# A sparse 3x3 convolution: TensorE's loop body cut to two blocks, input rows copied into two fixed tiles, both images in one add

## The chip, the cores and the metric

The kernel runs on one core of one Trainium2 chip. The metric is the device time of one execution in microseconds (us), from several executions; a profile is taken of one of them. The page of a profile gives a span, from the first to the last instruction on the core, and the device time of the same execution is a little longer than that span.

The engines are called by the names of the profile: PE is TensorE (matmuls; PEld are its weight loads), DVE is VectorE, ACT is ScalarE, POOL is GpSimd, SP is SyncE, which here only issues DMAs. SBUF is the on-chip memory, PSUM the eight accumulator banks that PE writes. A name with a q at its end (SPq, PEq, DVEq) is an engine's sequencer, which issues instructions, waits on semaphores and runs loops.

## The reference

The input holds 16 images of 64 channels and 64x64 points, the weight 128x64x3x3, about 90% of it zero. The output is a plain 3x3 convolution with a border of zeros, in float32:

```python
x_pad = np.pad(x, ((0, 0), (0, 0), (pad, pad), (pad, pad)), mode='constant')
...
if weight[co, ci, kh, kw] != 0:
    output[b, co] += weight[co, ci, kh, kw] * x_pad[b, ci, kh:kh+h, kw:kw+w]
```

The kernel treats the weight as dense. The input is 16.8 MB in float32, the output 33.6 MB, and all of both passes through the core's DMA engines.

## The kernel before

**Tiling.** Two images lie side by side on the 128 partitions (64 channels each): a pair. There are NP = 8 pairs. A block is 16 output rows of a pair, so there are NB = 32 blocks, four to a pair. PE works on both images of a block at once: each product is issued as two matmuls with 64 rows of the array each (`n = 0, 1` in `product`), one for each image, and they run side by side.

**The arithmetic.** Write G0, G1, G2 for the three rows of the filter. For an even output row r and the odd row below it, with S = x[r] + x[r+1] and P = G1·S:

- even row: P + (G2 − G1)·x[r+1] + G0·x[r−1]
- odd row: P + (G0 − G1)·x[r] + G2·x[r+2]

Each G stands for three taps, shifted by one column (`KW_ORDER`). So a block needs three products: P (3 taps), "even" (6 taps) and "odd" (6 taps), 15 taps times two images, 30 matmuls of 8 rows by 64 columns. The weight combinations G21 = G2 − G1 and G01 = G0 − G1 are made at the start (lines 228 and 231). Two blocks, b = 0 and 16 (`is_direct`), are instead computed directly, with 18 taps and no P. A matmul at the upper or lower edge of an image leaves one row out (`lo`, `hi` in `product`).

**Who does what for a block.** POOL makes S from two row sets of the input tile (line 190, tile `s`, four of them). PE computes P into two PSUM banks, even into two, odd into two; the eight banks are used in rotation (`bank`, six for each block, line 114). ACT copies P out of PSUM into SBUF, one copy for each image (line 214, tile `pc`). DVE adds P to even and odd and writes the output tile, four adds of 128x512 for each block: even and odd for each image (line 244, tile `o`). Three output tiles of a pair each are used in turn.

**Loops.** The program of PE is a loop of 16 blocks (TURN = 16), run twice (line 302). All other engines have their 32 blocks written out. At the turn, PE takes 16 off its three semaphores (line 335), so that the same numbers serve again. The weights of PE's loop body are fixed addresses, so the input tiles have to lie at the same place each time round: four tiles `x` of one pair each (SLOTS = 4) are reused by pairs 4 to 7.

**Loads and stores.** POOL's queue issues the input loads, which turn float32 into bf16 on the way. The first half of pair 0 comes apart from these, as float32 from SP's queue (`x_head`, line 126), and is turned into bf16 by DVE and ACT (line 98). Pairs 1 to 3 are loaded at the start. The loads of pairs 4 to 7 stand between POOL's additions (`AT`, line 169) and wait until PE has used up the pair that held the tile before (`free`, line 165). SP issues a store of 4 MB when DVE has finished a pair (line 129); the last pair goes out as two halves (line 135). At the end SP waits for the last four stores (line 339).

**Start.** PE runs seven matmuls on zeros, the nine transposes of the weights, and seven more matmuls on zeros (`keep_busy`, line 257), then enters the loop. Block 0 needs the cast rows of `x_head` from DVE, and no S.

Semaphores that the prediction speaks of: `p`, `q` count finished products of PE; `e0`, `e1` count adds of DVE by which PE learns that banks are free; `s` counts POOL's additions; `o` counts finished blocks for SP.

Of the kernel before, what the change touches and what calls it, by code (L numbers as in the profile page):

```python
# [7 lines left out]
FP32 = mybir.dt.float32  # L8
BF16 = mybir.dt.bfloat16
# [8 lines left out]
def kernel(  # L18
# [11 lines left out]

    nc = tc.nc
# [6 lines left out]
    SLOTS = 4  # L38
    TURN = 4 * SLOTS
    HEAD = 32  # L40
    N_O = 3
    N_S = 4
    N_PC = 4
# [9 lines left out]
    xs = tiles(SLOTS, [128, H, W], BF16, "x")  # L53
    os = tiles(N_O, [C_OUT, 2, H, W], FP32, "o")
    ss = tiles(N_S, [128, 8, W], BF16, "s")
    pcs = tiles(N_PC, [128, 8, W], FP32, "pc")
# [7 lines left out]
    ps = [psum_pool.tile([128, 8, W], FP32, name=f"ps{k}") for k in range(8)]  # L64
# [19 lines left out]
    def is_direct(b):  # L84
        return b % TURN == 0

    def p_count(b):
        return 2 * sum(not is_direct(k) for k in range(b))

# [7 lines left out]
    def cast_x(copy, a, b):  # L97
        return copy(out=xs[0][:, a:b, :], in_=x_head[:, a:b, :])  # L98

    def wps(g):  # L100
        return ps[(2, 3, 6)[g]].rearrange("p a b -> p (a b)")[:, 0:384].rearrange("p (k c) -> p k c", k=3)
# [4 lines left out]
    def rows_of(b):  # L106
        p, r0 = b // 4, 16 * (b % 4)
        o = os[p % N_O]
        if is_direct(b):
            return [o[:, n, r : r + 8, :] for r in (r0, r0 + 8) for n in range(2)]  # L110
        return [o[:, n, r : r0 + 16 : 2, :] for r in (r0, r0 + 1) for n in range(2)]

    def bank(b, k):
        return ps[(6 * b + k) % 8]

    LAST = (5, 6, 7, 8)

    with tc.tile_critical(no_gpsimd_drain=True):  # L118
        with nc.Block(no_gpsimd_drain=True) as block:  # L119

            @block.sync
            def _(sp):
# [4 lines left out]
                for p in range(NP - 1):  # L127
                    after(
                        sp.dma_start(out=out_of(p), in_=os[p % N_O]), ("o", 4 * p + 4)
                    ).then_inc(S(f"st{p}"), 16)  # L130
                for h in range(2):
                    rows = slice(32 * h, 32 * h + 32)
                    p = NP - 1
# [4 lines left out]
                        ("o", 4 * p + 2 + 2 * h),  # L138
                    ).then_inc(S(f"st{p + h}"), 16)

            @block.gpsimd
            def _(gp):
                def load(p, a, b, *waits):
                    after(
                        gp.dma_start(out=xs[p % SLOTS][:, a:b, :], in_=pair(p)[:, a:b, :]), *waits  # L145
                    ).then_inc(S(f"x{p}_{a}"), 16)

                load(0, HEAD, H)
                gp.memset(ident, 0.0).then_inc(S("id"), 1)
# [10 lines left out]
                    ("id", 1),  # L160
                ).then_inc(S("id"), 1)
                for p in range(1, SLOTS):
                    load(p, 0, H)

                def free(p):
                    return ("q", 16 * p - 48)

                CUT = 24
                AT = {
                    5: [(4, 0, CUT, ("q", 8))],  # L170
                    7: [(4, CUT, H, free(4))],
                    11: [(5, 0, H, free(5))],
                    15: [(6, 0, H, free(6))],
                    19: [(7, 0, 32, free(7))],
                    23: [(7, 32, H)],
                }
                LANDED = {0: (), 4: ("x1_0",), 8: ("x2_0",), 12: ("x3_0",), 16: ("x4_0", "x4_24"),
                          20: ("x5_0",), 24: ("x6_0",), 28: ("x7_0",), 29: ("x7_32",)}
                for b in range(NB):
                    waits = [(name, 16) for name in LANDED.get(b, ())]  # L180
                    if b == 1:
                        waits += [("a", 6), ("x0_32", 16)]
                    if b - N_S >= 0 and not is_direct(b - N_S):
                        waits.append(("p", p_count(b - N_S) + 2))
                    if is_direct(b):
# [12 lines left out]
                    for l in AT.get(b, ()):  # L198
                        load(*l)
# [170 lines left out]
```

## Time and profile before

| what | value |
|---|---|
| device time, median of 3 runs | 127.46 us (127.19 to 128.62) |
| device time of the profiled execution | 127.58 us |
| its span | 125.8 us |
| first matmul of the main loop | 8.58 us after the span's start |
| a block of PE, from one P product to the next | 3.24 us inside an image |
| stores of a pair issued (SP) | at 23.55 us, then about every 12.9 us; the seventh at 101.04 |
| last two stores issued | 107.44 and 113.85 us |
| loads of pairs 4 to 7 issued (POOL) | 22.53, 35.34, 48.14, 60.95, 72.77 us (the second part of pair 4, pairs 5 and 6, the halves of pair 7) |
| DMA queue q1 (SP's: stores, weight, `x_head`) | 65.8% of the 16 DMA engines' time |
| DMA queue q0 (POOL's: cast loads) | 31.3% of it |

How to read what follows: the page cuts the span into 40 slices of 3.1 us and gives the busy share of each engine as a digit. In a list of groups or in a timeline, `x24` is a count, the number behind the start is how long the piece lasted, and the words behind an arrow are what the engine waited for. The bytes of a load that casts are counted as they arrive, in bf16, at half of what is read. A DMA's "us to landing" runs from its issue to the semaphore that tells of its end.

### The profile page before, as it was taken

Reading aid. Unit: us, or ns where it says so; the run is one execution under the profiler, and the core shown is the slowest. Engines: PE = TensorE matmul, PEld = TensorE weight load, DVE = VectorE, ACT = ScalarE, POOL = GpSimd, SP = SyncE. Lnnn points to the kernel's source line nnn. Section 1 sums busy time; section 2 is a strip of 40 time slices with the busy share of each in tenths; the row PEclk is TensorE's granted clock in tenths of the full one; section 3 lists DMA queues with packets and bytes.
Section 4 is the critical chain, followed back from the end, with each engine's and each line's share of the span. In section 5 each row is a group of like instructions: output and inputs, shape, how many; then the busy total and the mean of one; then the engine's idle time right before and its main releaser. Section 6 shows DMA issues by size and latency. Waiting matters only on the chain.

```text
span 125.8 us, 2448 instructions
## 1 busy us (share of the span) xinstructions
PE 110.5 (88%) x995; PEld 58.1 (46%) x995; DVE 85.3 (68%) x137; ACT 36.7 (29%) x67; POOL 41.0 (33%) x48
## 2 busy tenths in 40 slices
PE   5989999999999999999999999999999999970000
PEld 2435555555555555555555555555555555530000
DVE  0346777877787778777868878877877787771000
ACT  4540333333333333333023333333333333330000
POOL 5409673533353332333523343333333200000000
PEclk9999999999999999999999999999999999999555
DMA  3999999999999999999999999999999999999980
GB/s 90 375 225 219 219 211 211 201 159 381 429 438 294 326 313 409 391 310 300 386 401 344 359 438 387 345 380 438 427 422 438 427 432 427 425 412 425 422 372 21
DMA packets 4184, 42.85 MB, mean 341 GB/s; under 512 B 337, under 2 KB 337, under 8 KB 1105
## 3 DMA queue, kind: packets, MB, share of 16 engines
q1 hardware_dynamic: 2736, 34.90, 65.8%
q0 software_dynamic: 1440, 7.86, 31.3%
q8 instruction: 4, 0.07, 0.2%
q14 instruction: 4, 0.02, 0.0%
HBM read 17.07 MB, written 33.55 MB: 402 GB/s over the span
## 4 chain that ended last, share of the span: by engine, by line
PE 82%; DMA 5%; DVE 1%; issue 1%; DVEq 0%; SPq 0%
PE ps L290 82%; DMA x_head<-in_x_dram 5%; DVE o L244 1%; DVEq L119 0%; DVE x L98 0%; SPq L123 0%; SPq L365 0%; SPq L118 0%
## 5 line engine op out<-in xcount | busy, mean ns | idle before, releaser
L290 PE MATMUL ps<-x,wT 64*128 64x504 bf16 (+3 forms) x792 | 89.9, 374 | 0.5 <-DVE x L98 0.5
L244 DVE TENSOR_TENSOR o<-ps,pc 128x512 f32<-128x512 f32 x120 | 76.8, 686 | 19.4 <-PE ps L290 19.2
L290 PEld LDWEIGHTS ps<-x,wT 64*128 64x128 bf16 x792 | 45.2, 94 | 40.1 <-issue 1.0
L214 ACT COPY pc<-ps 128x512 f32<-128x512 f32 x60 | 32.2, 589 | 69.4 <-PE ps L290 69.4
L190 POOL TENSOR_TENSOR s<-x 128x512 bf16<-128x512 bf16 x30 | 34.5, 1153 | 49.8 <-PE ps L290 43.4
L290 PE MATMUL ps<-s,wT 64*128 64x512 bf16 (+1 forms) x180 | 24.9, 377 | 0.0
L290 PEld LDWEIGHTS ps<-s,wT 64*128 64x128 bf16 x180 | 10.3, 94 | 8.8
L145 POOL DMA_DIRECT2D x<-in_x_dram x10 | 5.7, 574 | 7.3 <-PE ps L290 6.3
L240 DVE COPY o<-ps 128x512 f32<-128x512 f32 x8 | 5.2, 686 | 2.5 <-PE ps L290 2.5
L257 PE MATMUL ps<-idle_rhs 128*128 128x512 bf16 x14 | 5.6, 570 | 1.4 <-DVE idle_rhs L220 1.4
L257 PEld LDWEIGHTS ps<-idle_rhs 128*128 128x128 bf16 x14 | 1.8, 137 | 3.9 <-issue 2.4
L95 DVE CAST w_bf<-w_sb 128x192 bf16<-128x192 f32 (+1 forms) x4 | 1.1, 352 | 2.6 <-DMA w_sb<-in_weight_dram 2.6
L98 DVE CAST x<-x_head 128x576 bf16<-128x576 f32 x1 | 0.5, 460 | 2.9 <-DMA x_head<-in_x_dram 2.9
L98 ACT CAST x<-x_head 128x576 bf16<-128x576 f32 (+1 forms) x2 | 1.5, 804 | 1.7 <-DMA x_head<-in_x_dram 1.7
L95 ACT ACT_TABLE_LOAD x1 | 1.3, 1283 | 0.9 <-SPq L118 0.9
L262 PE MATMUL ps<-ident,w_bf 128*128 128x128 bf16 x9 | 1.3, 309 | 0.0
L262 PEld LDWEIGHTS ps<-ident,w_bf 128*128 128x128 bf16 x9 | 0.8, 132 | 1.1 <-DVE w_bf L95 1.1
L95 ACT CAST w_bf<-w_sb 128x64 bf16<-128x64 f32 (+1 forms) x2 | 0.7, 420 | 1.7 <-DMA w_sb<-in_weight_dram 1.7
L220 DVE MEMSET idle_rhs<- 128x256 uint32 x1 | 0.3, 272 | 1.1 <-SPq L118 1.1
L228 DVE TENSOR_TENSOR wT<-ps,wT 128x384 bf16<-128x384 f32 x1 | 0.6, 558 | 0.1
L206 ACT CAST wT<-ps 128x384 bf16<-128x384 f32 x1 | 0.5, 478 | 0.4 <-PE ps L262 0.4
L205 ACT CAST wT<-ps 128x384 bf16<-128x384 f32 x1 | 0.5, 478 | 0.4 <-PE ps L262 0.4
(9 smaller groups left out, 2.3 us busy)
## 6 DMA issues: line engine op xcount, KB each, us to landing
out_dram<-o SPq DMA_DIRECT2D x7, 4096.0 KB, 19.2
x<-in_x_dram POOLq DMA_DIRECT2D x5, 1024.0 KB, 15.3
out_dram<-o SPq DMA_DIRECT2D x2, 2048.0 KB, 11.3
x<-in_x_dram POOLq DMA_DIRECT2D x3, 512.0 KB, 12.2
x_head<-in_x_dram SPq DMA_DIRECT2D x1, 1024.0 KB, 6.6
x<-in_x_dram POOLq DMA_DIRECT2D x1, 640.0 KB, 10.9
x<-in_x_dram POOLq DMA_DIRECT2D x1, 384.0 KB, 9.8
w_sb<-in_weight_dram SPq DMA_DIRECT2D x1, 288.0 KB, 2.9
```

The lines of the kernel that those rows point to most:

```text
L95: return copy(out=w_bf4[:, g, a:b, :], in_=w_v[:, k : k + b - a, :])
L98: return copy(out=xs[0][:, a:b, :], in_=x_head[:, a:b, :])
L145: gp.dma_start(out=xs[p % SLOTS][:, a:b, :], in_=pair(p)[:, a:b, :]), *waits
L190: gp.tensor_tensor(out=ss[b % N_S], in0=xt[:, r0 : r0 + 16 : 2, :], in1=xt[:, r0 + 1 : r0 + 16 : 2, :], op=ADD,),
L205: after(act.copy(out=wT[:, G1], in_=wps(G1)), ("t", 1)).then_inc(S("a"), 1)
L214: act.copy(out=pcs[(2 * b + n) % N_PC], in_=bank(b, n)),
L228: dve.tensor_tensor(out=wT[:, G01], in0=wps(G0), in1=wT[:, G1], op=SUB), ("a", 3), ("d", 7)
L240: add = dve.tensor_copy(out=rows, in_=bank(b, (0, 1, 4, 5)[k]))
L244: add = dve.tensor_tensor(out=rows, in0=bank(b, 2 + k), in1=pcs[(2 * b + k % 2) % N_PC], op=ADD)
L257: mm = pe.matmul(idle_ps, idle_rhs[:, 0:128], idle_rhs, start=True, stop=True)
L262: mm = pe.matmul(wps(g)[:, j, :], w_bf[:, g, C_IN * j : C_IN * (j + 2)], ident, start=True, stop=True)
L290: mm = pe.matmul(dst[n][:, lo:hi, c_lo:c_hi], tap(g, kw, n), src[q, a:e:step, c_lo + kw - 1 : c_hi + kw - 1], start=(i == 0), stop=(i == l ...
```

## The change

The input no longer lives in four reused tiles: one tile `xs` holds all eight pairs in bf16, each with a row of zeros above and below (`H + 2` rows). The load of pair p needs no free tile; its first part of pair 4 is issued at the start, and the later ones still stand between POOL's additions, one block earlier in the list each, with one wait (for pair 0's last add) ahead of the second part of pair 4.

PE does not read `xs`. For each block ACT copies the 18 rows that the block needs into one of two fixed tiles, `win0` and `win1`, two blocks ahead of PE (`window`). So PE's loop body is two blocks (TURN = 2), run 16 times, with no direct blocks and no rows left out at the edges. The rows of blocks 0, 1 and a row of 2 come from the float32 `x_head`, which is not cast apart any more; POOL makes S of blocks 0 and 1 from it too.

PSUM is four tiles of two banks: P has two of them in turn, even has one and odd has one. ACT copies P of both images with one instruction, DVE adds both images with one instruction (128x1024), so DVE has two adds for each block instead of four. The semaphores are cut down: `r` counts DVE's steps at the start and finished pairs; `e` and `o` count its adds; `x` counts finished windows.

```diff
-    SLOTS = 4
-    TURN = 4 * SLOTS
+    TURN = 2
...
-    xs = tiles(SLOTS, [128, H, W], BF16, "x")
+    xs = pool.tile([128, NP, H + 2, W], BF16, name="xs")
+    win = tiles(2, [128, 18, W], BF16, "win")
...
-    ps = [psum_pool.tile([128, 8, W], FP32, name=f"ps{k}") for k in range(8)]
+    ps_p = [psum_pool.tile([128, 2, 8, W], FP32, name=f"ps_p{k}") for k in range(2)]
+    ps_e = psum_pool.tile([128, 2, 8, W], FP32, name="ps_e")
+    ps_o = psum_pool.tile([128, 2, 8, W], FP32, name="ps_o")
...
+                load(4, 0, CUT)
+                for _ in range(16):
+                    gp.nop()
+
                 AT = {
-                    5: [(4, 0, CUT, ("q", 8))],
-                    7: [(4, CUT, H, free(4))],
-                    11: [(5, 0, H, free(5))],
-                    15: [(6, 0, H, free(6))],
-                    19: [(7, 0, 32, free(7))],
-                    23: [(7, 32, H)],
+                    6: (4, CUT, H, ("r", R_OF[0])),
+                    10: (5, 0, H),
+                    14: (6, 0, H),
+                    18: (7, 0, 32),
+                    22: (7, 32, H),
                 }
...
+                    if b >= 2:
+                        waits.append(("p", b - 1))
+                    if b < 2:
+                        src = x_head[:, r0 : r0 + 16, :]
                     else:
+                        src = xs[:, p, r0 + 1 : r0 + 17, :]
...
+                def window(b):
+                    p, r0 = b // 4, 16 * (b % 4)
+                    parts = [(xs[:, p, r0 : r0 + 18, :], 0, [])]
...
+                    if b >= 2:
+                        parts[0][2].append(("q", HEAD_Q + 2 * (b - 2) + 2))
+                    for k, (src, a, waits) in enumerate(parts):
+                        copy = after(
+                            act.copy(out=win[b % 2][:, a : a + src.shape[1], :], in_=src), *waits
+                        )
+                        if k == len(parts) - 1:
+                            copy.then_inc(S("x"), 1)
+
+                window(0)
+                window(1)
+                for b in range(NB):
+                    after(act.copy(out=pcs[b % 2], in_=ps_p[b % 2]), ("p", b + 1)).then_inc(S("c"), 1)
+                    if b + 2 < NB:
+                        window(b + 2)
...
+                for b in range(NB):
+                    p, r0 = b // 4, 16 * (b % 4)
+                    for k, src in enumerate((ps_e, ps_o)):
+                        waits = [("q", HEAD_Q + 2 * b + k + 1)]
+                        if k == 0:
+                            waits.append(("c", HEAD_C + b + 1))
+                            if b % 4 == 0 and p >= N_O:
+                                waits.append((f"st{p % N_O}", 16 * (p // N_O)))
                         after(
+                            dve.tensor_tensor(
+                                out=os[p % N_O][:, :, r0 + k : r0 + 16 : 2, :], in0=src, in1=pcs[b % 2], op=ADD
                             ),
                             *waits,
+                        ).then_inc(S("eo"[k]), 1)
+                    if b % 4 == 3 or b == NB - 3:
+                        dve.memset(mark, 0.0).then_inc(S("r"), 1)
...
+                pe.wait_ge(S("r"), HEAD_R)
...
-                with pe.Fori(0, NP // SLOTS, 1):
+                with pe.Fori(0, NB // TURN, 1):
                     for l in range(TURN):
...
+                        xw = win[l]
+                        product(ps_p[l], [(ss[l], G1, 0, 1)], "p", [("s", l + 1), ("x", l + 1)])
+                        product(ps_e, [(xw, G21, 2, 2), (xw, G0, 0, 2)], "q", [("e", l + 1)])
+                        product(ps_o, [(xw, G01, 1, 2), (xw, G2, 3, 2)], "q", [("o", l + 1)])
+                    for name in ("s", "x", "e", "o"):
                         pe.sem_inc(S(name), -TURN)
```

## The prediction

> **What bounds the kernel now.** I read the page's slices first, then the chain of waits, the DMA's landings in three stretches, and last the engines' timeline around PE's loop turn.
>
> ```profile
> span 125.8 us, 2448 instructions
> ...
> PE   5989999999999999999999999999999999970000
> ...
> PEclk9999999999999999999999999999999999999555
> DMA  3999999999999999999999999999999999999980
> ...
> HBM read 17.07 MB, written 33.55 MB: 402 GB/s over the span
> ```
>
> PE is busy in every slice from the third to the 36th, and so are the DMA engines, from the second to the 38th. Two resources are full at once. The chain of waits and two stretches of the table by windows (columns: length, busy of PE, PEld, DVE, ACT, POOL, granted clock, DMA share, GB/s) tell which ends last.
>
> ```profile
> 8.58 102.74 PE ps L290 x960
> ...
> 111.92 1.30 DVE o L244 x2
> ...
> 102.00:105.00 3.00, 3.00 (x31) 1.61 (x28) 2.34 (x5) 1.07 (x2) 0.00 (x0) 1.00 1.00 426
> ...
> 114.00:117.00 3.00, 0.00 (x0) 0.00 (x0) 0.00 (x0) 0.00 (x0) 0.00 (x0) 0.90 1.01 426
> 117.00:120.00 3.00, 0.00 (x0) 0.00 (x0) 0.00 (x0) 0.00 (x0) 0.00 (x0) 0.50 1.02 429
> ```
>
> The chain puts 82% on PE, but it ends at 113.8 us with the last add; the other 12 us are the stores, at the same 426 GB/s as while PE worked. 50.6 MB at 426 GB/s are 119 us, and the DMA starts at about 2 us: the DMA engines set the end, and PE matters only where it hands over a store too late. How late is too late is in the issues by stretch (store 5, then 6, then the last half):
>
> ```profile
> out_dram<-o SPq DMA_DIRECT2D x1, 4096.0 KB, 16.2
> ...
> out_dram<-o SPq DMA_DIRECT2D x1, 4096.0 KB, 13.5
> ...
> out_dram<-o SPq DMA_DIRECT2D x1, 2048.0 KB, 10.5
> ...
> w_sb<-in_weight_dram SPq DMA_DIRECT2D x1, 288.0 KB, 2.9
> ```
>
> The weight, with nothing ahead of it, needs 2.9 us for 0.29 MB, of which 0.7 is moving: 2.2 us of fixed latency. A store of 4.19 MB with nothing ahead would land 9.8 + 2.2 = 12.0 us after its issue, the last half 7.1. So store 6 (issued at 101.04) waited 1.5 us behind store 5, the last half (113.85) 3.4, and store 5 itself 4.2. **The reserve is 1.5 us, at store 6.** What comes later than that lengthens the kernel one for one; what comes earlier gains nothing.
>
> **The change part by part.** *PE's work.* 32 x 30 = 960 matmuls against 972. But blocks at an edge no longer leave a row out: before, two direct blocks took 3.81 us (8.58 to 12.39), the edge blocks 3.16, the others 3.24 (57.29 to the next P product inside an image). 2 x 3.81 + 14 x 3.17 + 16 x 3.24 = 103.8 us; after, 32 x 3.24 = 103.7. Nothing is won.
>
> *Start.* Before, PE began at 8.58, after one cast of `x_head` on DVE (landed 7.98, 0.46 us). After, block 0 waits for POOL's S and ACT's window, both from `x_head`. POOL: the row with bf16 inputs is 1153 ns; float32 inputs are in no row, and I take the same (end 9.2). ACT: casts of 576 and 896 elements took 672 and 935 ns, 0.82 ns an element; 17 rows are 1088 elements, 1.09 us (end 9.1). With the 0.14 us from DVE's cast to PE, PE begins at 9.3: **+0.7 us**. DVE's weight steps (three of 0.55 us) no longer stand behind the cast and are done by about 7.2. The extra load at POOL and its nops fall into idle time (POOL is idle from 4.4). PE now idles 1.3 us after its zeros instead of 0.5; should it return to the half rate of its first seven matmuls (0.43 us apart), that is up to 1.7 us more; the granted clock shows no such thing for the shorter gap, so I take 0.
>
> *DVE.* 512 elements took 686 ns, 384 took 558: 1.0 ns an element, so 1024 take 1.2 us; two rows (1.37) are the other end. Two for each block: 2.4 us against 2.59, inside 3.24.
>
> *ACT.* P of both images: 589 at 512, 478 at 384, so 1.03 us at 1024 (other end 1.18). The window, 18 rows of 1152 bf16 elements, continues 672 and 935 to 1.15 us (other end two of 576, 1.34). ACT goes from 1.07 to 2.1 us for each block: not a bound by itself. But the window of block b+2 waits for the end of block b, and P of b+1 is queued behind it on ACT, and DVE's even add behind that, and the single even tile, which PE wants in b+2, behind that.
>
> ```profile
> 57.29 0.83 PE L290 MATMUL ps<-s,wT 64*128 64x512 bf16 x6
> 57.94 6.50 PE L290 MATMUL ps<-x,wT 64*128 64x512 bf16 x60
> 58.14 1.07 ACT L214 COPY pc<-ps 128x512 f32<-128x512 f32 x2 [2.17 <-PE ps L290]
> ...
> 59.44 2.50 DVE L244 TENSOR_TENSOR o<-ps,pc 128x512 f32<-128x512 f32 x4 [0.66 <-PE ps L290]
> ```
>
> ACT starts 0.20 us after the next product has begun (57.94 to 58.14); the two copies overlap by 0.11 (2 x 0.59 − 1.07). The ring: 0.20 + window 1.15 − 0.11 + P 1.03 + hand-over 0.08 (ACT's last cast of `x_head` ends at 9.49, POOL starts at 9.57) + add 1.2 + 0.14 = 3.7 us, then even and odd 2.59: 6.3 us against 2 x 3.24 = 6.48. **It fits with 0.2 us to spare**, so I cost it at 0. The cover is the rest of block b+1; with all three upper ends the ring is 6.3 + 0.19 + 0.15 + 0.17 = 6.8, which would cost 0.3 us in each turn.
>
> *The turn.* PE's sequencer now turns 15 times instead of once. The page's groups for that code:
>
> ```profile
> L335 PEldq EVENT_SEMAPHORE  x6: 51/51/51, 58.2 to 110.4; - x6
> ...
> L302 PEldq COMPARE_BRANCH  x2: 76/152/229, 58.8 to 110.6; - x2
> ```
>
> Three subtractions and a taken branch take from 58.2 to 59.03, 0.83 us; PE itself has no gap there (60 matmuls from 57.94 in 6.50 us, across the turn at 60.43), because the sequencer was 2.2 us ahead. The Trainium skill ("Runtime: NRT & Kernel Launch", Instruction fetch mechanics) says that a taken branch out of the small window of fetched code stalls until its page is fetched; the jump over 16 blocks shows no stall here, and a body of two blocks would make one less likely, so by the rule too the sum would be unchanged. After the change the sequencer is held at the odd product until DVE has emptied the one odd tile: 0.20 + 1.2, behind the even add, about 1.5 us into the block. To put out 60 matmuls and loads of a block it took from 56.89 (first add of the block before, P's banks free) to 58.2: 22 ns each, 24 are 0.5 us. Turn: 0.83 + 0.15 for a fourth subtraction + up to 0.2 for the two waits ahead of P. Sum 1.5 + 0.5 + 1.2 = 3.2 us, against the 3.24 that PE is busy. Ends: 0 (PE has no less work), and 0.3 with an add of 1.37 us, twice. I take **0.05 us for each turn**, nearest to the sum.
>
> *Sum.* Store 6 leaves after 28 blocks: 9.3 + 28 x 3.24 + 0.20 + 1.2 + 0.1 (marker) = 101.5, +0.5 us, with 14 turns of 0.05 +1.2 us. The reserve is 1.5: nothing remains. Store 0: 9.3 + 13.0 + 1.5 = 23.8 against 23.55. The loads leave up to 3.3 us later (pair 5 behind S of block 10 at 37.3 against 35.34); store 0 lands 18.5 us after its issue, at 42, and store 1 is queued from 36.8, so the DMA has work; bound 0 to 1 us. SP's end waits are as before. The execution with the profile took 127.58, the median is 127.46; I predict **127.6 us**.
>
> On the upside, the Trainium skill ("DMA: Bandwidth & Descriptors", Specifications) gives 435 GB/s as the ceiling of the fabric and about 358 as HBM's share for a core. The run's mean of 402 is above the second, so that limit doesn't hold here; by the first, 50.6 MB take 116.4 us, an estimate, some 2.4 less than at 426.
>
> **The rivals.** *Exposed turn (slower).* If the sequencer doesn't get ahead again in a block, each turn leaves a gap. For it: the single even and odd tiles tie the sequencer to DVE, where eight rotating banks let it run. Against: the sum just fits. At 0.25 us, store 6 is 0.5 + 3.5 − 1.5 = 2.5 us too late: 130.1. It decides from 0.16 us a turn, where the loss reaches 1%.
>
> *The ring ACT, DVE, PE (slower).* At the upper ends, 0.3 us a turn: 0.5 + 4.5 − 1.5 = 3.5, so 131.1. For it: ACT's window is new and its bf16 form is in no row; against: all three rows extend on straight lines.
>
> *A hungry DMA.* Later loads leave the queues empty once, or the cold clock at the start: 0.5 to 1 us, 128.3; still within 1%.
>
> *Faster.* Only DMA time can give it. Idle shares in the body (0.96 in 27 to 30 us, 0.98 in 39 to 42) add up to some 0.2 us: 127.3. Less than 126.2 needs a higher rate, for which nothing in the profile speaks. That DVE's busy time falls from 85 to about 80 us is real and worth nothing.
>
> **How the numbers follow.** Forecast, no loss beyond the reserve: 0.47. Hungry DMA or cold start: 0.10. Exposed turn: 0.22. Ring: 0.16. Faster by DMA: 0.05. About 1%, 1.3 us, is what a measurement tells from no change (the three runs differ by that much). The two slower cases can be small; I give 0.02 of them to "same", and 0.01 of the faster case: faster 0.04, same 0.60, slower 0.36. The range goes from 126.9 (0.2 of DMA gain and the spread of the runs below the median) to 130.5, beyond the middle of the slower cases, which leaves out about 0.15 above and 0.04 below. The forecast alone spans 127.0 to 128.5.
>
> **What would show it.** Right: PE's first product at 9.3, DMA share at 1.00 up to store 6, blocks 3.24 us apart at every turn, a store 6 issued before 102.5. Wrong, exposed turn: PE idle every second block before a P product, with no releaser but issue. Wrong, ring: PE waiting for DVE ahead of each even product, ACT's window over 1.2 us. In both, a DMA share under 1 after 100 us. A store's landing that falls to 12.0 us is the sign that the reserve is gone.

## The result and the profile after

The changed kernel takes 126.21 us, the kernel before, measured beside it, 127.33 us: a ratio of 0.9885, 95% interval [0.9837, 0.9932]. It is 1.1% faster. I had predicted 127.6 us, with a range from 126.9 to 130.5 and a chance of 0.04 for faster; a gain of this size was what I had thought the profile could not bear.

The profiled execution took 126.21 us against 127.58, 1.37 us less. Here is its page first: PE's and the DMA's slices, the bytes moved in each slice, and the share of POOL's queue (q0).

```profile
span 124.4 us, 2437 instructions
...
PE   5949999999999999999999999999999999992000
...
DMA  3999999999999999999999999999999999999991
GB/s 85 375 225 213 211 219 219 239 438 338 332 363 432 308 329 324 387 353 345 298 379 408 321 369 427 413 367 348 433 421 432 427 384 427 458 390 416 413 419 71
...
q0 software_dynamic: 1440, 7.86, 30.6%
...
HBM read 17.07 MB, written 33.55 MB: 407 GB/s over the span
```

The rows of GB/s and of q0 on the page of before, which the prediction did not show:

```profile
GB/s 90 375 225 219 219 211 211 201 159 381 429 438 294 326 313 409 391 310 300 386 401 344 359 438 387 345 380 438 427 422 438 427 432 427 425 412 425 422 372 21
...
q0 software_dynamic: 1440, 7.86, 31.3%
```

The same loads, the same bytes, but they held the 16 DMA engines for 31.3% of 125.8 us before and 30.6% of 124.4 after: 39.4 against 38.1 us, 1.3 us less. The place is the eighth and ninth number of the GB/s row, 22 to 28 us: 201 and 159 before, 239 and 438 after. (A load that casts is counted at half of what it reads, so a stretch of loads alone at full rate shows about 215.) The table by windows makes it sharper; its last two columns are the DMA share and GB/s. Before, then after:

```profile
24.00:27.00 3.00, 3.00 (x32) 1.58 (x29) 2.58 (x4) 0.96 (x2) 1.16 (x2) 1.00 1.14 171
```

```profile
24.00:27.00 3.00, 3.00 (x32) 1.35 (x30) 2.30 (x2) 1.99 (x2) 1.28 (x2) 1.00 1.09 402
...
99.00:102.00 3.00, 3.00 (x32) 1.37 (x28) 2.19 (x4) 2.06 (x2) 1.15 (x1) 1.00 0.88 377
102.00:105.00 3.00, 3.00 (x32) 1.36 (x28) 2.22 (x2) 2.05 (x2) 1.15 (x1) 1.00 1.01 426
```

Before, the engines are called fully busy (1.14) and move 171 where loads alone move 215. That is not a DMA that waits; it is one that works slowly, and a busy share cannot show it. In the list of packets (a packet is one record of the trace; a load has 128 of them, one for each partition), the 5120-byte packets of pair 4's second load took 542 ns on average before and 398 after, and the first packet of store 0 came 4.4 us after its issue before (23.55 to 27.95), 1.5 us after it now (23.16 to 24.64). The issues of that load (POOL) and of store 0 (SPq) have changed places, before and then after:

```profile
22.53 0.57 POOL L145 DMA_DIRECT2D x<-in_x_dram  x1 [1.58 <-PE ps L290]
...
23.55 0.40 SPq L129 DMA_DIRECT2D out_dram<-o  x1
```

```profile
23.16 0.40 SPq L118 DMA_DIRECT2D out_dram<-o  x1
...
23.57 0.57 POOL L134 DMA_DIRECT2D xs<-in_x_dram  x1
```

I added up the bytes of all packets, read or written, by time: the changed kernel gains 1.05 us between 25 and 28 us, keeps it to 100 us, and gives 0.3 us back ahead of store 6 (the share of 0.88 in the second line).

The other gain lies behind the last packet. From there to the end of the span before took 1.92 us, now 1.44. The rows for the code after the last wait (POOL's sequencer: count, shortest, median and longest in ns, first and last start in us), before and then after:

```profile
L365 POOLq EVENT_SEMAPHORE  x4: 17/17/17, 124.5 to 125.7; - x4
L365 POOLq DRAIN  x3: 40/169/882, 114.8 to 125.5; - x3
...
L365 POOLq EVENT_SEMAPHORE_RANGE_CLEAR  x1: 244/244/244, 125.3 to 125.3; - x1
```

```profile
L343 POOLq EVENT_SEMAPHORE  x4: 17/17/17, 123.7 to 124.3; - x4
L343 POOLq DRAIN  x3: 40/107/882, 114.9 to 124.2; - x3
...
L343 POOLq EVENT_SEMAPHORE_RANGE_CLEAR  x1: 178/178/178, 124.0 to 124.0; - x1
```

From POOL's first step to its last it was 1.17 us (124.53 to 125.70) and is 0.68 (123.66 to 124.34). Of that, 0.07 us is the clearing of fewer semaphores, 0.06 a shorter drain, and 0.36 a pause between the first two steps: 0.448 us before, 0.085 after.

So the 1.37 us are 0.88 of DMA (last packet 123.88, now 123.00) and 0.48 of ending. Neither stands in the prediction. What did stand there, turns, ring and windows, behaved as it was reckoned. The timeline of after across the loop's turn (start, length, engine), and the waits of PE:

```profile
57.22 0.81 PE L292 MATMUL ps_p<-s,wT 64*128 64x512 bf16 x6
57.48 1.15 ACT L211 COPY win<-xs 128x1152 bf16<-128x1152 bf16 x1 [1.23 <-PE ps_o L292]
...
58.54 1.00 ACT L219 COPY pc<-ps_p 128x1024 f32<-128x1024 f32 x1
...
59.65 1.23 DVE L248 TENSOR_TENSOR o<-ps_e,pc 128x1024 f32<-128x1024 f32 x1 [0.94 <-ACT pc L219]
...
60.47 0.81 PE L292 MATMUL ps_p<-s,wT 64*128 64x512 bf16 x6
```

```profile
PE ps_p L292 <- POOL s L178: 1.6, 1, 1.6
...
PEld ps_e L292 <- DVE o L248: 0.8, 3, 0.5
```

Block after block comes at 3.24 us (57.22, 60.47), turn or no turn. Of the 31 steps from block to block 30 are 3.24 or 3.25 us. The waits of PE in the body that show are 0.8 us of its weight loads, in three places, and 0.2 in a fourth; the longest makes one block 3.38 us (86.40 to 89.78).

### The profile page after: what moved, and what is told of

Its sections match the earlier page's. It is cut to its first block, busy times and chain, and to the rows that moved or that the text cites. A ratio compares the mean times of both kernels' runs of the same rounds, so it can differ in the third digit from the quotient of the medians.

```text
span 124.4 us, 2437 instructions
## 1 busy us (share of the span) xinstructions
PE 109.6 (88%) x983; PEld 49.1 (39%) x983; DVE 79.2 (64%) x83; ACT 69.3 (56%) x71; POOL 43.0 (35%) x48
## 3 DMA queue, kind: packets, MB, share of 16 engines
q0 software_dynamic: 1440, 7.86, 30.6%
## 4 chain that ended last, share of the span: by engine, by line
PE 84%; DMA 5%; POOL 1%; DVE 1%; SPq 0%; issue 0%; DVEq 0%
PE ps_e L292 33%; PE ps_o L292 33%; PE ps_p L292 17%; DMA x_head<-in_x_dram 5%; POOL s L178 1%; DVE o L248 1%; SPq L112 0%; SPq L343 0%; SPq L107 0%; DVEq L108 0%
## 5 line engine op out<-in xcount | busy, mean ns | idle before, releaser
L248 DVE TENSOR_TENSOR o<-ps_e,pc 128x1024 f32<-128x1024 f32 x32 | 39.2, 1225 | 31.2 <-ACT pc L219 22.9
L178 POOL TENSOR_TENSOR s<-xs 128x512 bf16<-128x512 bf16 x30 | 34.5, 1150 | 58.0 <-PE ps_p L292 58.0
L211 ACT COPY win<-xs 128x1152 bf16<-128x1152 bf16 (+2 forms) x31 | 34.7, 1121 | 34.2 <-PE ps_o L292 34.2
L292 PE MATMUL ps_e<-win,wT 64*128 64x504 bf16 (+1 forms) x384 | 46.8, 377 | 0.0
L292 PE MATMUL ps_o<-win,wT 64*128 64x504 bf16 (+1 forms) x384 | 46.8, 377 | 0.0
L248 DVE TENSOR_TENSOR o<-ps_o,pc 128x1024 f32<-128x1024 f32 x32 | 38.9, 1216 | 0.1
L219 ACT COPY pc<-ps_p 128x1024 f32<-128x1024 f32 x32 | 32.2, 1006 | 1.8 <-PE ps_p L292 1.8
L292 PEld LDWEIGHTS ps_o<-win,wT 64*128 64x128 bf16 x384 | 18.9, 94 | 22.6 <-DVE o L248 0.2
L292 PEld LDWEIGHTS ps_e<-win,wT 64*128 64x128 bf16 x384 | 18.8, 94 | 22.8 <-DVE o L248 0.8
L292 PE MATMUL ps_p<-s,wT 64*128 64x504 bf16 (+1 forms) x192 | 26.0, 377 | 1.6 <-POOL s L178 1.6
```

Source lines behind the costliest of these rows:

```text
L178: gp.tensor_tensor(out=ss[b % 2], in0=src[:, 0:16:2, :], in1=src[:, 1:16:2, :], op=ADD),
L211: act.copy(out=win[b % 2][:, a : a + src.shape[1], :], in_=src), *waits
L219: after(act.copy(out=pcs[b % 2], in_=ps_p[b % 2]), ("p", b + 1)).then_inc(S("c"), 1)
L248: dve.tensor_tensor(out=os[p % N_O][:, :, r0 + k : r0 + 16 : 2, :], in0=src, in1=pcs[b % 2], op=ADD),
L292: mm = pe.matmul(dst[:, n, :, c_lo:c_hi], tap(g, kw, n), src[q, first : first + 7 * step + 1 : step, c_lo + kw - 1 : c_hi + kw - 1], start ...
```

## The experiments

Sixteen kernels were run. All numbers of "loads left" below are worked out the same way: the bytes of the loads issued ahead of store 0 whose packets have not begun when store 0 is issued, as read in float32, over 425 GB/s. "Pause" is POOL's 0.448 or 0.085 us.

**The order of the second load of pair 4 and store 0.** In the kernel before that load waits for PE's last product of pair 0 and goes ahead of store 0; in the changed kernel it waits for DVE's last add, as the store does, and goes behind. Each kernel gets the other's order.

```diff
# b_store_first, from the kernel before
-                    7: [(4, CUT, H, free(4))],
+                    7: [(4, CUT, H, ("o", 4))],
# a_load_first, from the changed kernel
-                    6: (4, CUT, H, ("r", R_OF[0])),
+                    5: (4, CUT, H),
```

> The kernel before, with one edit: the second load of pair 4 waits for DVE's fourth finished block (the same event that lets store 0 go) and so is issued with store 0, not 1.0 us ahead of it. Theory order: the change won about 1.1 us because in the kernel before the DMA engines worked badly from 25 to 28 us (201 and 159 GB/s in the slices there, against 219), while a load issued ahead of store 0 held them alone; expected a time 1.0 us below before (ratio about 0.992), store 0's landing down from 18.5 to under 16 us. Rival early first part: the gain comes from the first part of pair 4 being queued at the start and not at 16 us; then this edit gives nothing (ratio 1.000, landing still 18 us). Rival end only: the gain is at the program's end; nothing here either.

> The changed kernel, with the second load of pair 4 moved one block earlier and without its wait, so that it is issued at about 20.4 us, ahead of store 0 (23.2). Theory order: the poor stretch of DMA comes back, time up by 0.7 to 1.1 us (about 127.0 to 127.3), store 0's landing from 15 to over 17 us. Rival early first part: no change (126.2).

b_store_first: 127.01 us against 127.50 (0.9967 [0.9943, 0.9991]); a_load_first: 127.30 (0.9988 [0.9963, 1.0013]), against 126.03 for the changed kernel on the same chip. One line of the kernel before is worth 0.5 us, half of the 1.0 that was expected, and store 0 landed 19.0 us after its issue, not under 16; one line of the changed kernel gives back 1.3 of its 1.5 us. The stretch from 24 to 27 us, of b_store_first and of a_load_first:

```profile
24.00:27.00 3.00, 3.00 (x31) 1.60 (x28) 2.33 (x4) 1.07 (x2) 1.79 (x2) 1.00 1.08 386
```

```profile
24.00:27.00 3.00, 3.00 (x32) 1.36 (x28) 2.11 (x3) 2.06 (x2) 1.15 (x1) 1.00 1.10 151
```

The poor stretch is there where the load goes first, and gone where it goes second. PE, DVE and ACT keep their counts in both.

**How much load is queued, without the order.**

```diff
# a_pair4_whole: no second load of pair 4 at all (the wait for its landing goes down to 16)
-                load(4, 0, CUT)
+                load(4, 0, H)
...
-                    6: (4, CUT, H, ("r", R_OF[0])),
# a_cut40: 40 rows of pair 4 at the start in place of 24
-    CUT = 24
+    CUT = 40
```

> The changed kernel with pair 4 loaded whole at the start, so no load is issued between 5 and 36 us, and store 0 meets a load queue that is full until about 28 us. Theory order: a load's descriptors written while another load drains are what costs; with none written, no poor stretch, time as the changed kernel (126.2) or less. Rival meeting: the poor stretch is any store that begins while loads alone hold the engines; then it is here too, just before 28 us, and the time is 127 or more.

> The changed kernel with the first part of pair 4, loaded at the start, cut at row 40 and not 24: when store 0 is issued (23 us), loads are queued for about 1.2 us longer (until some 26.4 us and not 25.1). Theory meeting: what is lost grows with the loads that are still queued when store 0 is issued (none lost at 24 rows, 0.6 us with the whole pair); at 40 rows 0.2 to 0.4 us (126.4 to 126.6). Rival order alone: only a load issued just ahead of the store costs; time as the changed kernel, 126.2.

a_pair4_whole took 127.23 us (0.9995 [0.9969, 1.002]), a_cut40 126.52 (0.9912 [0.9884, 0.9939]). In a_pair4_whole the pause of 0.445 us was back too, so 0.8 of its 1.2 us over the changed kernel are the DMA's. In a_cut40, whose time is 0.3 to 0.5 us over the changed kernel's (126.21 and, in a repeat, 126.03), the order is that of the changed kernel and the poor stretch is there all the same:

```profile
24.00:27.00 3.00, 3.00 (x32) 1.34 (x30) 2.12 (x3) 2.06 (x2) 1.14 (x1) 1.00 1.00 150
```

So it is not the order of two instructions as such, but what is still queued when store 0 is issued.

The loads' own packets show when the slowing begins. In the changed kernel, between 18 and 33 us, none of them took over 1.1 times what is usual for its size. In a_cut40 (store 0 issued at 22.71 us) the first such packet began at 23.53, in a_pair4_whole (22.59) at 24.53, and in a_pair4_whole_pool1 (below; 23.99) at 25.00: 0.8 to 1.9 us after the issue, and 2.0 to 3.6 us ahead of the store's first packet. What the slow packets took too long, over 16 engines, is 1.06, 0.70 and 1.17 us in these three, 1.14 in the kernel before and 1.19 in a_load_first: about what their DMA is behind at 32 us in the table below.

**The same order, the store later.** Is pair 4's second load slow by itself? Here it still goes first, and only store 0 waits for one more block.

```diff
# b_store0_late, from the kernel before
-                        sp.dma_start(out=out_of(p), in_=os[p % N_O]), ("o", 4 * p + 4)
+                        sp.dma_start(out=out_of(p), in_=os[p % N_O]), ("o", 4 * p + 4 + (p == 0))
# a_load_first_store0_late, from a_load_first
-                    if b % 4 == 3 or b == NB - 3:
-                        dve.memset(mark, 0.0).then_inc(S("r"), 1)
+                    if b % 4 == 3 or b in (4, NB - 3):
+                        dve.memset(spare if b == 4 else mark, 0.0).then_inc(S("r"), 1)
```

(R_OF and the last two stores' counts go up by one in the second.)

> The kernel before, but store 0 waits for one more block, so it is issued at about 26.8 us instead of 23.55; the second load of pair 4 still goes first, and nothing else is moved. Theory (a store issued while several us of loads are queued slows both): fewer than 1.5 us of loads are left at 26.8, the stretch of 25 to 28 us runs at the rate of a load alone (about 215 GB/s as the page counts them, against 171), its packets of 5120 bytes take about 400 ns instead of 542, and the time falls by 0.5 to 1 us to 126.5 to 127.0. Rival (the load of pair 4 is slow by itself): the stretch stays at 171 GB/s and 542 ns, and with store 0 later still the time is 127.5 or more.

> The kernel a_load_first (the second load of pair 4 ahead of store 0, 127.3 us), with store 0 issued one block later, at about 26.4 us. Theory (meeting of store and queued loads): packets of 5120 bytes at about 400 ns instead of 467, no poor stretch at 24 to 28 us, and the time back at 126.0 to 126.4 us, as the changed kernel, although the order of load and store is that of the kernel before. Rival (the load is slow by itself, or the order alone counts): 127.2 us or more.

b_store0_late: 127.11 us (0.9956 [0.9933, 0.9979]), a gain of 0.4 us from issuing one store one block later; the packets of 5120 bytes took 415 ns. The time is 0.1 us above the expected range; but PE had begun early in the profiled execution (7.54 us), so the store left at 25.68 and not 26.8, with 2.5 us of loads ahead. a_load_first_store0_late: 126.89 (0.9947 [0.9921, 0.9972]). Its profiled execution, at 126.22 us, did what was expected: 401 ns, and the full rate of loads alone:

```profile
24.00:27.00 3.00, 3.00 (x32) 1.34 (x30) 2.31 (x3) 1.98 (x2) 1.15 (x1) 1.00 1.06 204
...
28.00:31.00 3.00, 3.00 (x32) 1.37 (x28) 2.11 (x3) 2.06 (x2) 1.15 (x1) 1.00 1.02 429
```

But its executions lie between 126.2 and 127.7 us, and their median missed the expected 126.0 to 126.4. The load is not slow by itself; that the whole 1.2 us come back by delaying the store, the median does not bear out. A little of the slowing is there without a store, too: 0.15 us in all, from 23.54 us on, while both loads of pair 4 were queued.

The profiles side by side, one execution each; the lead is in bytes moved at 32 us, in us, against a repeat of the changed kernel (a_no_nop):

| kernel | loads left at store 0 (us) | first packet of store 0 after its issue (us) | lead at 32 us |
|---|---|---|---|
| a_pe_late (below) | 0.4 | 0.9 | −1.39 |
| a_pe_late_cut40 (below) | 1.2 | 1.1 | −0.20 |
| changed kernel | 1.6 | 1.5 | −0.18 |
| a_load_first_store0_late | 1.6 | 1.5 | −0.13 |
| b_store_first | 1.9 | 2.0 | −0.15 |
| b_store0_late | 2.5 | 2.3 | −0.41 |
| a_cut40 | 3.1 | 4.1 | −1.11 |
| a_pair4_whole_pool1 (below) | 3.6 | 4.6 | −1.01 |
| b_pe_late (below) | 3.7 | 4.9 | −1.86 |
| before | 4.2 | 4.4 | −1.18 |
| a_load_first | 4.9 | 4.8 | −1.15 |
| a_pair4_whole | 4.9 | 3.9 | −0.58 |

From 1 to 2 us left, next to nothing is lost (the other five kernels, all with 1.4 to 2.0, stand between −0.06 and −0.23); from 3 us on, mostly 1.0 and more. With 0.4 left the DMA runs dry, which is told below. It is no straight line, and a_pair4_whole falls out of it. Nor does the time follow the lead in every kernel: a_cut40 is 1.1 us behind at 32 us, and its median is only 0.3 to 0.5 us longer.

**The loop body.** The changed kernel with its old length of PE's loop, 16 blocks run twice.

```diff
-    TURN = 2
+    TURN = 16
...
-                        xw = win[l]
-                        product(ps_p[l], [(ss[l], G1, 0, 1)], "p", [("s", l + 1), ("x", l + 1)])
+                        xw = win[l % 2]
+                        product(ps_p[l % 2], [(ss[l % 2], G1, 0, 1)], "p", [("s", l + 1), ("x", l + 1)])
```

> The changed kernel with PE's loop body written out for 16 blocks and run twice, as before (the two fixed tiles used alternately); all else as changed. Theory order: the loop body has no part in the gain; time 126.2 as the changed kernel, PE's blocks 3.24 us apart as there. Rival code: the four transfers of 16 KB of instructions that the kernel before had and the changed one has not load a DMA engine by some 0.9 us each, and the slowest DMA engine ends the kernel; then 0.5 us or more come back (126.7 or more), with four transfers on the queue of instructions.

126.02 us (0.9866 [0.98, 0.9932]), as the changed kernel. The queue that carries instructions is back in the page, and PE's products stand where they stood:

```profile
q8 instruction: 4, 0.07, 0.2%
```

```profile
57.20 0.81 PE L292 MATMUL ps_p<-s,wT 64*128 64x512 bf16 x6
...
60.44 0.81 PE L292 MATMUL ps_p<-s,wT 64*128 64x512 bf16 x6
```

PE's loop body of two blocks, the first thing that the title names, is worth nothing in either direction. The fixed tiles and the joint add have no run of their own.

**The pause at the end.** The first two kernels here were to separate it from the DMA's part by the 16 `nop`s on POOL.

```diff
# a_no_nop; b_store_first_nop16 adds the same lines to b_store_first
-                for _ in range(16):
-                    gp.nop()
```

> The changed kernel without the 16 empty instructions on POOL. At the end POOL answers 0.09 us after SP's last wait in the changed kernel and 0.45 us in the kernel before. Theory fetch: the 16 instructions shift POOL's code so that the pause goes; without them it comes back, 0.3 to 0.4 us (126.6). Rival nothing: the pause has another cause, and the time stays at 126.2.

> The kernel before with the second load of pair 4 issued with store 0 (as in b_store_first) and, besides, 16 empty instructions on POOL at the start. Theory place of code: POOL's pause of 0.45 us after SP's last wait comes from where its code happens to lie (it was there in the kernel before, in b_store_first and in a_pair4_whole, with other counts of POOL instructions, and not in the changed kernel with or without the 16); moving the code by 16 instructions takes it away: about 126.6 (b_store_first 127.0 less 0.4). Rival: the pause belongs to the kernel before's semaphores or tiles; it stays, and the time is 127.0.

126.03 us (0.9881 [0.9855, 0.9907]) and 127.05 (0.9951 [0.9915, 0.9988]). These runs settle nothing: the page counts 2437 instructions with the `nop`s and without, and 2448 likewise in the other pair, so these instructions leave nothing in the program (some later variants of the changed kernel leave the `nop`s out, too). The runs serve as repeats: 126.21 and 126.03, 127.01 and 127.05. What did differ was the count of POOL's instructions in the trace: 74 in the kernel before, in b_store_first and in a_pair4_whole, all with the pause; 75 in the changed kernel. (The expectations give these counts four higher: 78, 79 and 80.) So the next three kernels add one instruction that does leave something, a memset.

```diff
# b_store_first_pool1, a_pair4_whole_pool1, a_pool1: behind the loads at the start
+                gp.memset(spare, 0.0)
```

> The kernel before with the second load of pair 4 behind store 0 (as in b_store_first), and one more instruction on POOL, a memset of one column behind the first loads (79 instructions on POOL, as many as in the changed kernel, in place of 78). Theory (the length of POOL's program decides whether it pauses 0.45 us between the last wait on SP and the clearing of the semaphores): the pause falls to 0.09 us, the stretch from the last DMA packet to the end of the span from 1.92 to about 1.56 us, the time from 127.0 to 126.65 us. Rival (the pause belongs to the program of before, with its wider list of semaphores and its loop of 16 blocks): the pause stays at 0.445 us and the time at 127.0 us.

> The changed kernel with pair 4 loaded whole at the start, as in a_pair4_whole, and the same extra memset on POOL, so that POOL has 79 instructions again and not 78. Theory (length of POOL's program): pause 0.09 us instead of 0.445, end sequence 1.48 instead of 1.84, time 126.85 instead of 127.2 us; what is left above 126.1, 0.7 us, is then the cost of a load that is still queued when store 0 is issued. Rival: the pause stays at 0.445 us and the time at 127.2.

> The changed kernel with the extra memset on POOL: 80 instructions. If only one certain length is free of the pause (an alignment), it comes back here: 0.445 us, 126.45 us. If the pause is gone from 79 on, it stays at 0.09 us and the time at 126.1 us.

b_store_first_pool1: 126.63 us (0.9933 [0.9894, 0.9971]), 0.4 less than without, as expected. POOL's steps at the end, in b_store_first and with one memset more:

```profile
L365 POOLq EVENT_SEMAPHORE  x4: 17/17/17, 123.8 to 125.0; - x4
```

```profile
L368 POOLq EVENT_SEMAPHORE  x4: 17/17/17, 124.0 to 124.7; - x4
```

1.2 us became 0.7; the pause fell from 0.445 to 0.086, with 244 ns of clearing as before. a_pair4_whole_pool1 lost the pause too (0.086), and took 127.06 us (0.9944 [0.9912, 0.9976]), 0.17 less and not 0.36. a_pool1, with 76 instructions, kept the short pause (0.083) at 126.21 (0.987 [0.9816, 0.9924]). In all 18 profiles it is so: 0.445 to 0.448 us in the six kernels with 74 instructions on POOL, 0.083 to 0.086 in the twelve with 75 or 76. An instruction that does nothing for the result takes 0.36 us off the end of the program. Whether its number or its place in POOL's program does it, and why, is not shown.

**The reserve at store 6.** In a_store6_halves the seventh store goes out as two halves, the first at 94.43 us (the marker of the block is set there as well). In a_pe_late twelve more matmuls on zeros hold PE's first product back.

```diff
# a_store6_halves
-                for p in range(NP - 1):
+                for p in range(NP - 2):
...
+                for p in (NP - 2, NP - 1):
+                    for h in range(2):
# a_pe_late; b_pe_late has keep_busy(14) at the same place
-                keep_busy(7)
+                keep_busy(19)
                 pe.sem_inc(S("e"), 1)
```

> The changed kernel without the 16 empty instructions, with store 6 issued as two halves, the first two blocks earlier (about 94.6 us). In the changed kernel store 5 ends before store 6 has begun and the DMA share falls to 0.93 from 99 to 102 us. Theory reserve: that gap, about 0.3 us, is won: 125.7 against 126.03 for the same kernel with store 6 whole. Rival slowest engine: the gap only hits DMA engines that are done early anyway, and the one that ends last gains nothing: 126.0.

> The changed kernel with twelve more matmuls on zeros before the loop, so that PE's first product starts about 1 us later (about 9.5 us) and every store leaves 1 us later. If the reserve at store 6 that the prediction reckoned (1.5 us before; store 6 left at the same time here) holds, the time stays within 0.3 us of 126.1. If what the DMA gained at 25 to 28 us has used the reserve up, as the gap at store 6 suggests (first packet of store 6 0.6 us ahead of the last of store 5), the lead falls by most of the 1 us there and the time is 126.8 to 127.1 us.

a_store6_halves: 126.21 us (0.9878 [0.9815, 0.994]). The share at 99 to 102 us was 0.97, but the repeat of the changed kernel with store 6 whole (a_no_nop) has 0.98 there and not 0.88, so the halves need not have done it. The trace does not name a packet's engine; laid end to end, the packets make 16 rows, and the middle one of these ended at 121.33 us (121.93 in the changed kernel, 121.67 in the repeat), the last at 122.96 (123.00 and 122.78). The kernel's time is that of the slowest engine; what the others won brought nothing.

a_pe_late: 127.52 us (0.9995 [0.9968, 1.0023]), above both expectations. With PE's first product at 9.81 us, 1.1 later than in a_pool1, which ran beside it, the time is 1.3 us longer. For a delay of this size there is no reserve at all; and the loss is early, in two stretches in which the DMA runs dry:

```profile
24.00:27.00 3.00, 3.00 (x32) 1.38 (x28) 2.18 (x4) 1.82 (x3) 1.41 (x3) 1.00 0.91 314
...
28.00:31.00 3.00, 3.00 (x30) 1.36 (x28) 2.35 (x2) 1.82 (x3) 0.85 (x2) 1.00 0.97 279
```

**Both edits together.** If the loads left at store 0 decide, a late PE and 40 rows at the start must cancel.

```diff
# a_pe_late_cut40
-    CUT = 24
+    CUT = 40
...
-                keep_busy(7)
+                keep_busy(19)
                 pe.sem_inc(S("e"), 1)
```

> The changed kernel with PE about 1 us later (as a_pe_late, 127.5 us) and 40 rows of pair 4 loaded at the start in place of 24 (as a_cut40, 126.5 us). Theory (the loads left when store 0 is issued decide): 1.2 to 1.8 us of them are left at about 24 us, as in the changed kernel, so the two edits cancel between 24 and 31 us, and only the gap ahead of store 6 is left of PE's delay: 126.5 to 126.9 us, below a_pe_late. Rival (each edit has its own cost): the losses add up, 127.8 us or more.

> The kernel before with seven more matmuls on zeros ahead of the loop: PE and all stores about 1 us later. By the reserve that the prediction reckoned (1.5 us, at store 6) nothing is lost: 127.3 to 127.7 us. Theory (loads left at store 0): 4.2 us of loads are left in the kernel before, 1 us less of them here, so the poor stretch gets shorter if anything, and the time is 127.0 to 127.6 us. If PE's start is passed on one for one as in the changed kernel, it is 128.3 us or more.

a_pe_late_cut40: 127.50 us (0.9998 [0.9972, 1.0024]). Neither expectation held. At store 0 the edits do cancel: 1.2 us of loads left, a lead of −0.20 at 32 us. But the DMA then runs dry one store later, at 36 to 39 and 42 to 45 us:

```profile
36.00:39.00 3.00, 3.00 (x30) 1.37 (x28) 2.18 (x4) 2.06 (x2) 1.66 (x2) 1.00 0.74 294
...
42.00:45.00 3.00, 3.00 (x32) 1.36 (x28) 2.12 (x3) 2.06 (x2) 1.15 (x1) 1.00 0.91 229
```

By 48 us it is 1.8 us behind. In these two kernels, what PE hands over late at the start is lost at store 0 or at store 1, about one for one; no later slack gives it back.

b_pe_late: 127.83 us (1.0024 [1.0004, 1.0044]), 0.3 us for a first product at 9.20 us, which is 0.6 later than in the profile of the kernel before and 1.2 to 1.7 later than in those of its other variants (7.54 to 7.97). That is between the two expectations: some of PE's delay, half of it at most, is passed on in the kernel before too, and fewer loads left (3.7) did not shorten the poor stretch. Its profiled execution took 128.85 us, at the far end of its own runs (from 127.63), so its row of the table is a weak one.

## Why the prediction failed, step by step

**"50.6 MB at 426 GB/s": a constant rate.** This is the step that failed. I measured the rate at 102 to 120 us, where stores run alone, and took the busy share of 1.0 elsewhere as proof that the DMA had nothing to give. The sum itself was open: a start at 2 us and 119 us make 121, the last packet came at 123.88, and I did not ask where the 2.9 us between them went; 1.14 of them are the loads' slow packets from 24.6 us on, while store 0 waited behind them. I searched the share for idle time, found 0.2 us, and wrote that for a higher rate "nothing in the profile speaks". The page's row of GB/s spoke: 201 and 159 where the five slices ahead show 211 to 225. With the byte count doubled for loads, that is a deficit of (215 − 171) / 215 × 3 us = 0.6 us in the window of 24 to 27 us alone. The gain measured by bytes is 1.05 us between 25 and 28 us, of which 0.88 reached the last packet.

**"The loads leave up to 3.3 us later … bound 0 to 1 us."** I priced the moved loads for their delay and gave them only a loss. That the second load of pair 4 passes from ahead of store 0 to behind it was in the diff and in the issue times (22.53 and 23.55), and I did not put the two queues beside each other. b_store_first and a_load_first show what the move is worth: 0.5 and 1.3 us of gain, where I had put a loss of 0 to 1.

**"SP's end waits are as before."** Wrong by 0.48 us in the profiled execution. The waits are as before, but what follows them is not: 0.36 us of pause that hangs on one instruction of POOL, and 0.13 of semaphores and drain. That the 0.13 would shrink I could have read from the change ("the semaphores are cut down") and the row of 244 ns; the pause I could not.

**"The reserve is 1.5 us, at store 6"; "What comes earlier gains nothing."** The sum of latencies was sound as far as it went: store 6 landed 12.5 us after its issue (it was 13.5), close to the 12.0 at which I called the reserve gone. But a reserve has to be sought at every store. a_pe_late and a_pe_late_cut40 show that in the changed kernel a delay of 1.1 us or more finds none at stores 0 and 1, and b_pe_late loses some too.

**Start: "+0.7 us".** Right, though the number 9.3 was not: from the landing of `x_head` to PE's first product it was 0.60 us (7.98 to 8.58) and is 1.38 (7.21 to 8.59). The landing itself came 0.77 us earlier in this execution, which hid it. In the other profiles with an unchanged start it shows: the first product came at 7.54 to 7.97 us in the variants of the kernel before, and at 8.02 to 8.67, once at 9.42, in those of the changed one.

**DVE, ACT, ring, turn.** The terms held:

```profile
L248 DVE TENSOR_TENSOR o<-ps_e,pc 128x1024 f32<-128x1024 f32 x32 | 39.2, 1225 | 31.2 <-ACT pc L219 22.9
...
L211 ACT COPY win<-xs 128x1152 bf16<-128x1152 bf16 (+2 forms) x31 | 34.7, 1121 | 34.2 <-PE ps_o L292 34.2
...
L219 ACT COPY pc<-ps_p 128x1024 f32<-128x1024 f32 x32 | 32.2, 1006 | 1.8 <-PE ps_p L292 1.8
...
L178 POOL TENSOR_TENSOR s<-x_head 128x512 bf16<-128x512 f32 x2 | 2.5, 1270 | 2.4 <-DMA x_head<-in_x_dram 2.4
```

1225 ns for the add (1.2 us was reckoned), 1.15 for a full window (1.15), 1.01 for P (1.03), 1.27 for S from float32 (1.15, the one that was short). The turn's sum of 3.2 us against 3.24 was taken as a risk of 0.05 us a turn and two rivals of 0.38 together; with 16 rounds of the loop and with two (a_turn16) there is no difference. The third rival, a hungry DMA, did not happen in the changed kernel, but it was near: a PE that starts 1.1 us later meets it (a_pe_late). The Trainium skill ("Runtime: NRT & Kernel Launch", Instruction fetch mechanics) says that code comes in blocks of 16 KiB fetched ahead and that a taken branch out of the window stalls. The four instruction transfers of 0.07 MB with 16 blocks, and none with two, agree with the first; a stall shows with neither.

**What stays open.** Shown is that the gain at store 0 comes and goes with the loads queued there, and the one at the end with an instruction on POOL; by what mechanism a waiting store slows the loads, or POOL pauses, is not. The parts shown in the kernel before add up to 0.5 (order at store 0) and 0.4 (pause): b_store_first_pool1 at 126.63. a_pool1, the changed kernel with one memset more, ran beside it at 126.21. Of the 0.4 between them, 0.07 is the clearing of semaphores (244 and 178 ns). The rest would fit the same meeting at store 1, since b_store_first loses some 0.35 us of its lead between 36 and 40 us, where pair 5's load still goes 1 us ahead of store 1; that was not tried. No kernel of the study was faster than the changed one by more than repeats differ.

## What to carry to other kernels

A DMA share of 1.0 says that the engines are held, not that they move what they can: read the GB/s row beside it, double what casting loads are counted at, and ask for every slow stretch which two queues meet there. When a change moves a load past a store, write both queues down in order with the bytes left at each issue, since in the profiles here 1 to 2 us of queued loads were free, and 3 to 5 us mostly put the DMA 1 us or more behind (0.3 to 1.3 us of the kernel's time). And look for the reserve at each handover, the first ones above all, not only at the last.

## What was not expected of the hardware

- A store's first packet came about when the loads queued ahead would have run out at full rate: 4.4 us after its issue with 4.2 us of loads left, 1.5 with 1.6, 2.3 with 2.5 (about 1 us off in a_cut40, a_pair4_whole, a_pair4_whole_pool1 and b_pe_late). In most kernels at most 0.3 us of them were in fact left by then, in b_pe_late 0.5, in the kernel before 0.8, in a_load_first 1.2, in a_pair4_whole 1.8. The Trainium skill ("DMA: Bandwidth & Descriptors", Queues, rings and completion order) says that each DMA engine goes round between the queues that have work and drains a whole packet of one before it switches, where a packet is a group of some 9 to 17 descriptors. A load has 128 packets in the trace, so an engine's share of it, 8 if they are spread evenly, may go as one such packet, and a wait for the rest of one load fits. In a_load_first, though, the packets of a second load began 2.2 us after the store's issue (25.08 us) and the store's first at 27.64, so there the store waited for a share of a second load as well; whether the two go as one group no run shows. Why the loads themselves slow down meanwhile (542 ns a packet for 398) no run here shows either.
- The DMA engines do not end together. In the changed kernel the middle one of the 16 rows of packets ended at 121.93 us, the last at 123.00; in the kernel before 122.34 and 123.88.
- POOL pauses 0.45 us between its first two steps after the last wait in the kernels with 74 instructions on POOL, and 0.08 to 0.09 us in those with 75 and 76.
